# Two mixers of a tuned TensorE-bound kernel: the softmax by four heads at a time, and ten taps and a split behind the first scores

## The chip, the core and the metric

The kernel runs on one core of a Trainium2 chip. The metric is the device time of one execution in microseconds. Before the change three runs took 2920.37, 2922.01 and 2922.98 us, so the median is 2922.01 us. The engines are named as in the profile: PE is TensorE (PEld its weight loads), DVE is VectorE, ACT is ScalarE, POOL is GpSimd, SP is SyncE, which issues most of the weight transfers.

## What is computed

The program is two networks in a row: a block of depth 2 (each layer: feed-forward, mixer, feed-forward) on 512 tokens of width 1024, and then a second block with a scan, a gated mixer and sixteen experts. The change touches the mixer of the first block alone, which runs twice. Cut to what matters:

```python
u = x @ w_in
u_conv, u_lru, q, k, v = jnp.split(u, [o1, o2, o3, o4], axis=-1)
y_conv = _conv_module(u_conv, ...)      # gate, 31 causal taps, layernorm, silu
y_lru = _recurrent(u_lru, ...)          # short conv, gates, scan, gelu gate
y_attn = _swa(q, k, v, ...)             # 8 heads, blocks of 128, window 128
return jnp.concatenate([y_conv, y_lru, y_attn], axis=-1) @ w_out

# _swa, per block of 128 queries, over this block of keys and the one before
s = einsum('bnqgrd,bnkgd->bngrqk', qb, kb) * (HEAD_DIM ** -0.5) + band_bias
s = where(valid, s, -1e30)
p = softmax(concatenate([s, sink], axis=-1))[..., :-1]
o = einsum('bngrqk,bnkgd->bnqgrd', p, vb)
```

The output projection needs all three parts, and the four query blocks of the attention are independent of each other.

## The kernel before

Every large product runs on TensorE as three matmuls of split operands (high by high, high by low, low by high). Weights come through one stream in order of use: SP loads 512 KB pieces into a ring of four buffers (`raw`); ACT copies a piece to its high part (`whl`, line 81) and DVE subtracts to get the low part (line 82), which frees the buffer. The stream also carries `ada_w`, weights of the second network, which need no split: eight steps of `mod` (line 853), each of two pieces and four matmuls, are spread over the mixer as filler, and a piece's buffer is free when its second matmul has read it.

The mixer goes as follows. Fourteen projections (`pj`) give the inputs. DVE works off a list of 62 taps of the convolution (`tap`, line 372, in place on `acc`) in portions that `drain(n)` takes, between the splits of q (`ql`, line 406), the recurrence (`hs`) and its split into the operand of the output projection (`split_to`, lines 631 and 632). Then come the four query blocks. `scores(b)` makes two pairs of score banks (`sc`, line 461; `rp` 0 holds heads 0 to 3, `rp` 1 heads 4 to 7); DVE adds the bias, and takes the maximum with the sink, head by head (line 468, tile `S`); then for all eight heads at once the negated maximum (471) and the sink's difference (472); ACT does eight exponentials with row sums (475) and the sink's (476); DVE adds and takes the reciprocal (477, 478); the heads are normalized by turns on DVE (484) and ACT (482). `pv(b)` transposes the heads (`tp`, 496) for each of the block's key blocks, has ACT copy group 0 (`pT`, 501) and DVE group 1 (`pT`, 499), multiplies by v (`yv`, 506, one instruction for each group), and splits the result (`xTh` on ACT, 511; `xTl` on DVE, 512). Block 0 has one key block, the others two. The convolution's layernorm (`conv_ln`: `cn`, `bn`, `mv`, a square root on ACT with its table load in `rs`, `nt`, `cb`, `yc`) and the last `pv` run beside the output projection (`down`, line 220, bank `dn`, 12 matmuls for each of its half steps).

The text of the program isn't the order of the engines: a scheduler orders each engine's instructions by its own estimates of their durations, and each engine then runs its list strictly as it stands; what it estimates wrong shows as a wait. The code calls `scores(0)`, `scores(1)`, `pv(0)`, `scores(2)`, `pv(1)`, `scores(3)`, the first steps of `conv_ln`, `pv(2)`, and leaves the rest of `conv_ln` and `pv(3)` to `down`.

Of the kernel before, what the change touches and what calls it, by code (L numbers as in the profile page):

```python
# [10 lines left out]
AF = mybir.ActivationFunctionType  # L11
OP = mybir.AluOpType
# [86 lines left out]
class Kernel:  # L99
# [237 lines left out]
    def mixer(self, l, st, pb, ln, nxt):  # L337
        nc, w = self.nc, self.w
# [77 lines left out]
        lru = {}  # L416
# [29 lines left out]
        def scores(b):  # L446
            k0 = 0 if b else 128
            ks = slice((b - 1) * 128 if b else 0, (b + 1) * 128)
            n = 256 - k0
            st = self.mp.tile([128, 5, 8], F32, tag="sm", name="sm", bufs=4)  # L450
            s = {}
            sink = self.sinks[:, l]
            bs = slice(b * 128, b * 128 + 128)
            for rp in range(2):
                ps = [self.ps("sc").rearrange("p (r k) -> p r k", r=2) for _ in range(2)]
                for rr in range(2):
                    for n_m in range(3):
                        for g in range(2):
                            hs = slice(g * 64, g * 64 + 64)
                            lq, rk = ((self.qh, self.kh), (self.qh, self.kl), (self.ql, self.kh))[n_m]  # L460
                            nc.tensor.matmul(ps[g][:, rr, :n], lq[hs, 2 * rp + rr, bs], rk[hs, ks], start=(n_m == 0),
                                             stop=(n_m == 2))
                for g in range(2):
                    t = mun(name="S").rearrange("p (r k) -> p r k", r=2)
                    for rr in range(2):
                        r = 2 * rp + rr
                        h = 2 * r + g
                        nc.vector.tensor_tensor_reduce(t[:, rr, k0:], ps[g][:, rr, :n], self.bias[:, r, g, k0:], 1.0,
                                                       sink[:, h:h + 1], op0=OP.add, op1=OP.max, accum_out=st[:, 0, h:h + 1])
                    s[rp, g] = t  # L470
            nc.vector.tensor_scalar(st[:, 1], st[:, 0], -1.0, None, op0=OP.mult)
            nc.vector.tensor_tensor(out=st[:, 2], in0=sink, in1=st[:, 0], op=OP.subtract)
            for h in range(8):
                sv = s[h // 4, h % 2][:, h // 2 % 2, k0:]
                nc.scalar.activation(sv, sv, AF.Exp, bias=st[:, 1, h:h + 1], accum_out=st[:, 3, h:h + 1])
            nc.scalar.activation(st[:, 2], st[:, 2], AF.Exp)
            nc.vector.tensor_tensor(out=st[:, 3], in0=st[:, 3], in1=st[:, 2], op=OP.add)
            nc.vector.reciprocal(st[:, 4], st[:, 3])
            for h in range(8):
                sv = s[h // 4, h % 2][:, h // 2 % 2, k0:]  # L480
                if h % 2:
                    nc.scalar.activation(sv, sv, AF.Copy, scale=st[:, 4, h:h + 1])
                else:
                    nc.vector.tensor_scalar(sv, sv, st[:, 4, h:h + 1], None, op0=OP.mult)
            sc[b] = s

        def pv(b):
# [86 lines left out]
        for r in range(4):  # L574
            pj(10 + r)
            post_q(r)
            self.drain(6)
            if r == 0:
                v_nat()
        for c in range(2):  # L580
            self.split_to(c, lru[c])
        per = PER
        run = lambda *gs: [0 for g in gs for _ in g]
        scores(0)
        self.drain(5)
        self.mod(per)
        scores(1)
# [1470 lines left out]
```

## Time and profile before

| | us |
|---|---|
| median of three runs | 2922.01 |
| the profiled execution | 2918.46 |
| its span, first to last instruction | 2916.7 |
| PE busy | 2863.8 (98%) |
| DVE busy | 1333.1 (46%) |
| ACT busy | 1004.5 (34%) |

A row of the timeline has a start in us from the span's start, a duration, engine, line, operation, tile written and read, shape and count; in brackets stands how long the engine was idle before it, and what ended that. Durations of successive instructions overlap, so the pace is the step from one start to the next. Matmuls of fp32 leave two records each, so `x4` in the trace is two instructions of the order. The first mixer's attention lies at 464 to 525 us, the second's 922.8 us later, at 1387 to 1448.

### The profile page before, as it was taken

Reading aid. Unit: us, or ns where it says so; the run is one execution under the profiler, and the core shown is the slowest. Engines: PE = TensorE matmul, PEld = TensorE weight load, DVE = VectorE, ACT = ScalarE, POOL = GpSimd, SP = SyncE. Lnnn points to the kernel's source line nnn. Section 1 sums busy time; section 2 is a strip of 40 time slices with the busy share of each in tenths; the row PEclk is TensorE's granted clock in tenths of the full one; section 3 lists DMA queues with packets and bytes.
Section 4 is the critical chain, followed back from the end, with each engine's and each line's share of the span. In section 5 each row is a group of like instructions: output and inputs, shape, how many; then the busy total and the mean of one; then the engine's idle time right before and its main releaser. Section 6 shows DMA issues by size and latency. Waiting matters only on the chain.

```text
span 2916.7 us, 35208 instructions
## 1 busy us (share of the span) xinstructions
PE 2863.8 (98%) x14404; PEld 2196.4 (75%) x14404; DVE 1333.1 (46%) x2259; ACT 1004.5 (34%) x1591; POOL 37.7 (1%) x63
## 2 busy tenths in 40 slices
PE   8999998999999999999899999999999999999998
PEld 7888885888888878888588888878878886544453
DVE  4223398533334333359653334778863453222223
ACT  4222355422224122344552223567742321100011
POOL 0000000000000000000100000000000000000000
PEclk9999999999999999999999999999999999999999
DMA  6432334333223354232633323232244357899998
GB/s 197 114 101 74 96 116 150 97 112 108 94 80 95 95 191 137 80 108 70 200 109 98 104 80 103 89 115 80 88 138 137 94 202 281 342 406 426 426 427 329
DMA packets 104257, 465.91 MB, mean 160 GB/s; under 512 B 12837, under 2 KB 13493, under 8 KB 79520
## 3 DMA queue, kind: packets, MB, share of 16 engines
q1 hardware_dynamic: 95936, 435.81, 41.7%
q0 software_dynamic: 6720, 23.13, 2.8%
q10 hardware_dynamic: 1440, 4.72, 0.4%
q8 instruction: 113, 1.85, 0.3%
q14 instruction: 48, 0.39, 0.0%
HBM read 457.73 MB, written 5.88 MB: 159 GB/s over the span
## 4 chain that ended last, share of the span: by engine, by line
PE 84%; DVE 7%; DMA 5%; ACT 2%; issue 1%; SPq 0%; DVEq 0%; ACTq 0%
PE dn L220 19%; PE pg L114 6%; PE pg L115 6%; PE pg L116 6%; PE pu L116 5%; PE pu L114 5%; PE pu L115 5%; DMA er<-in_eu 3%; PE ey L1671 3%; PE pj L115 3%; PE pj L116 3%; PE pj L114 3%; PE eu L1671 2%; PE eg L1671 2%; PE ga L1671 2%; PE wo L1455 2%
## 5 line engine op out<-in xcount | busy, mean ns | idle before, releaser
L82 DVE TENSOR_TENSOR whl<-raw,whl 128x1024 fp32r<-128x1024 f32 (+1 forms) x385 | 468.6, 1221 | 692.0 <-ACT whl L81 691.7
L81 ACT ACTIVATE whl<-raw 128x1024 fp32r<-128x1024 f32 (+1 forms) x385 | 405.9, 1056 | 659.8 <-PE pu L116 249.8
L220 PE MATMUL dn<-whl,hhl 128*128 128x512 f32 x2112 | 492.9, 395 | 0.0
L220 PEld LDWEIGHTS dn<-whl,hhl 128*128 128x128 f32 x2112 | 397.5, 188 | 92.3
L114 PE MATMUL pg<-xTh,whl 128*128 128x512 f32 x768 | 300.3, 391 | 0.0
L116 PE MATMUL pg<-xTh,whl 128*128 128x512 f32 x768 | 298.9, 389 | 0.0
L115 PE MATMUL pg<-xTl,whl 128*128 128x512 f32 x768 | 298.8, 389 | 0.0
L114 PE MATMUL pu<-xTh,whl 128*128 128x512 f32 x704 | 274.7, 390 | 0.7 <-ACT whl L81 0.7
L115 PE MATMUL pu<-xTl,whl 128*128 128x512 f32 x704 | 273.9, 389 | 0.0
L116 PE MATMUL pu<-xTh,whl 128*128 128x512 f32 x704 | 273.7, 389 | 0.0
L114 PE MATMUL pj<-xTh,whl 128*128 128x256 f32 (+1 forms) x688 | 230.7, 335 | 0.0
L116 PE MATMUL pj<-xTh,whl 128*128 128x256 f32 (+1 forms) x688 | 224.8, 327 | 0.0
L115 PE MATMUL pj<-xTl,whl 128*128 128x256 f32 (+1 forms) x688 | 224.5, 326 | 0.0
L114 PEld LDWEIGHTS pg<-xTh,whl 128*128 128x128 f32 x768 | 144.2, 188 | 36.8 <-issue 7.4
L116 PEld LDWEIGHTS pg<-xTh,whl 128*128 128x128 f32 x768 | 144.1, 188 | 30.3
L115 PEld LDWEIGHTS pg<-xTl,whl 128*128 128x128 f32 x768 | 144.2, 188 | 29.3
L290 ACT ACTIVATE sg<-pg 128x512 f32<-128x512 f32 x80 | 47.8, 597 | 320.8 <-PE pg L116 320.8
L114 PEld LDWEIGHTS pu<-xTh,whl 128*128 128x128 f32 x704 | 132.1, 188 | 28.6 <-ACT whl L81 1.1
L116 PEld LDWEIGHTS pu<-xTh,whl 128*128 128x128 f32 x704 | 132.2, 188 | 27.6
L115 PEld LDWEIGHTS pu<-xTl,whl 128*128 128x128 f32 x704 | 132.1, 188 | 27.5 <-issue 0.2
L293 DVE SCALAR_TENSOR_TENSOR h<-sg,pu 128x512 f32<-128x512 f32 x74 | 50.8, 687 | 198.2 <-PE pu L116 198.2
L115 PEld LDWEIGHTS pj<-xTl,whl 128*128 128x128 f32 x688 | 131.4, 191 | 10.9 <-issue 0.5
(483 smaller groups left out, 3855.3 us busy)
## 6 DMA issues: line engine op xcount, KB each, us to landing
raw<-in_wgu SPq DMA_DIRECT2D x176, 512.0 KB, 3.6
er<-in_eu SPq DMA_DIRECT2D x64, 1024.0 KB, 18.9
er<-in_eg SPq DMA_DIRECT2D x64, 1024.0 KB, 18.2
er<-in_ed SPq DMA_DIRECT2D x56, 1024.0 KB, 19.1
raw<-in_wd SPq DMA_DIRECT2D x88, 512.0 KB, 3.5
raw<-in_win SPq DMA_DIRECT2D x76, 512.0 KB, 3.6
raw<-in_ada_w SPq DMA_DIRECT2D x48, 512.0 KB, 4.7
raw<-in_wout SPq DMA_DIRECT2D x16, 512.0 KB, 4.6
```

The lines of the kernel that those rows point to most:

```text
L81: k.nc.scalar.activation(hi, r, AF.Copy)
L82: k.nc.vector.tensor_tensor(out=lo, in0=r, in1=hi.bitcast(F32), op=OP.subtract)
L114: mm(out, l[0], r[0], start=start, stop=False)
L115: mm(out, l[0], r[1], start=False, stop=False)
L116: mm(out, l[1], r[0], start=False, stop=stop)
L220: nc.tensor.matmul(banks[t, dh], l[:, s], r[:, dh * 512:(dh + 1) * 512], start=(u == 0 and n_l == 0), stop=(u == last and n_l == 2))
L290: nc.scalar.activation(sg, pg, AF.Silu)
L293: return nc.vector.scalar_tensor_tensor(h, sg, 0.5, pu, op0=OP.mult, op1=OP.mult)
L1455: nc.tensor.matmul(banks[t, dh], mg[k][l][:, s], wo[k][dh][r], start=(k == 0 and n == 0), stop=(k == 7 and n == 2))
L1671: return tc.keep_in_program_order(nc.tensor.matmul(*args, **kw))
```

## The change

The softmax of a block is now done inside the loop over `rp`, for four heads at a time: negated maximum, sink's difference, four exponentials, sum, reciprocal and normalization for heads 0 to 3 and again for heads 4 to 7. The portions that `drain` takes behind the four q projections go from 6, 6, 6, 6 to 6, 6, 0, 0, so ten taps are still on the list when `scores(0)` is called, and `split_to` of the recurrence is called behind `scores(0)`. Nothing else is changed; lines behind the loop move by two.

```diff
-            nc.vector.tensor_scalar(st[:, 1], st[:, 0], -1.0, None, op0=OP.mult)
-            nc.vector.tensor_tensor(out=st[:, 2], in0=sink, in1=st[:, 0], op=OP.subtract)
-            for h in range(8):
...
+                hs = slice(4 * rp, 4 * rp + 4)
+                nc.vector.tensor_scalar(st[:, 1, hs], st[:, 0, hs], -1.0, None, op0=OP.mult)
+                nc.vector.tensor_tensor(out=st[:, 2, hs], in0=sink[:, hs], in1=st[:, 0, hs], op=OP.subtract)
+                for h in range(4 * rp, 4 * rp + 4):
+                    sv = s[rp, h % 2][:, h // 2 % 2, k0:]
+                    nc.scalar.activation(sv, sv, AF.Exp, bias=st[:, 1, h:h + 1], accum_out=st[:, 3, h:h + 1])
+                nc.scalar.activation(st[:, 2, hs], st[:, 2, hs], AF.Exp)
+                nc.vector.tensor_tensor(out=st[:, 3, hs], in0=st[:, 3, hs], in1=st[:, 2, hs], op=OP.add)
+                nc.vector.reciprocal(st[:, 4, hs], st[:, 3, hs])
+                for h in range(4 * rp, 4 * rp + 4):
...
             post_q(r)
-            self.drain(6)
+            self.drain((6, 6, 0, 0)[r])
...
-        for c in range(2):
-            self.split_to(c, lru[c])
...
         scores(0)
+        for c in range(2):
+            self.split_to(c, lru[c])
         self.drain(5)
```

In the scheduled program PE, DVE and ACT change between the last q projection and the end of the attention, in the same way in both mixers; outside these stretches their orders are the same as before, and SP's is the same throughout.

**Block 0.** DVE at the last q split and the first scores (`ISA S,sm` is line 468 of one head, `acc` a tap, whose number of columns counts down to 482 for the last one), before:

```order
L406 SCALAR_TENSOR_TENSOR ql<-pj,qh 128x512
L372 SCALAR_TENSOR_TENSOR acc<-yin,pc,acc 128x488
L372 SCALAR_TENSOR_TENSOR acc<-yin,pc,acc 128x487
L372 SCALAR_TENSOR_TENSOR acc<-yin,pc,acc 128x486
L468 ISA S,sm<-sc,bias,sinks 128x128
L468 ISA sm 128x1
L372 SCALAR_TENSOR_TENSOR acc<-yin,pc,acc 128x485
```

DVE at the same place now, the q split first:

```order
L406 SCALAR_TENSOR_TENSOR ql<-pj,qh 128x512
L372 SCALAR_TENSOR_TENSOR acc<-yin,pc,acc 128x489
L372 SCALAR_TENSOR_TENSOR acc<-yin,pc,acc 128x488
L372 SCALAR_TENSOR_TENSOR acc<-yin,pc,acc 128x487
L468 ISA S,sm<-sc,bias,sinks 128x128
```

and at the end of the first four heads:

```order
L468 ISA sm 128x1
L372 SCALAR_TENSOR_TENSOR acc<-yin,pc,acc 128x486
L473 TENSOR_SCALAR sm<-sm 128x4
L474 TENSOR_TENSOR sm<-sinks,sm 128x4
L372 SCALAR_TENSOR_TENSOR acc<-yin,pc,acc 128x485
```

The q split stands one tap earlier, the recurrence's split still stands ahead of it, and of the ten taps five still stand ahead of the scores and five stand between and behind them. PE behind the scores of block 1 up to block 0's product with v, before:

```order
L853 MATMUL mod<-raw,cs 32x512 x9
L496 MATMUL tp<-ident,S 128x128 x7
L853 MATMUL mod<-raw,cs 32x512
L496 MATMUL tp<-ident,S 128x128
L853 MATMUL mod<-raw,cs 32x512 x6
L506 MATMUL yv<-pT,vn 64x512 x2
```

and now:

```order
L855 MATMUL mod<-raw,cs 32x512 x4
L498 MATMUL tp<-ident,S 128x128 x4
L855 MATMUL mod<-raw,cs 32x512
L498 MATMUL tp<-ident,S 128x128 x4
L855 MATMUL mod<-raw,cs 32x512 x8
L508 MATMUL yv<-pT,vn 64x512 x2
```

Five of the filler's matmuls that stood ahead of block 0's transposes now stand between or behind them.

**Block 2.** PE behind the scores of block 3 (`cn` the convolution's transposes, the first `tp` and `yv` those of block 2's first key block), before:

```order
L524 MATMUL cn<-ident,acc 128x128 x4
L496 MATMUL tp<-ident,S 128x128 x8
L506 MATMUL yv<-pT,vn 64x512
L524 MATMUL cn<-ident,acc 128x128 x2
L496 MATMUL tp<-ident,S 128x128
L524 MATMUL cn<-ident,acc 128x128 x2
L496 MATMUL tp<-ident,S 128x128 x7
L220 MATMUL dn<-whl,xTh 128x512 x2
```

and now:

```order
L526 MATMUL cn<-ident,acc 128x128 x4
L498 MATMUL tp<-ident,S 128x128 x8
L526 MATMUL cn<-ident,acc 128x128 x4
L508 MATMUL yv<-pT,vn 64x512 x2
L498 MATMUL tp<-ident,S 128x128 x8
L220 MATMUL dn<-whl,xTh 128x512
L508 MATMUL yv<-pT,vn 64x512
L220 MATMUL dn<-whl,xTh 128x512 x2
L508 MATMUL yv<-pT,vn 64x512
```

The second `yv` of block 2's first key block stood behind 17 matmuls of the output projection (not shown) and stands now ahead of all of them; the pair of its second key block stood behind 24 and stands behind one and three. ACT at this place (the first `pT` is block 1's second key block, the second one block 2's first; `S,sm` x8 are the exponentials of block 3), before:

```order
L501 ACTIVATE pT<-tp 128x512
L81 ACTIVATE whl<-raw 128x1024
L482 ACTIVATE S<-S,sm 128x256 x4
L511 ACTIVATE xTh<-yv 128x4x128
L81 ACTIVATE whl<-raw 128x1024 x2
L501 ACTIVATE pT<-tp 128x512
L81 ACTIVATE whl<-raw 128x1024
L475 ACTIVATE S,sm<-S,sm 128x256 x8
L476 ACTIVATE sm<-sm 128x8
L530 ACT_TABLE_LOAD
L530 ACTIVATE rs<-mv,eps_100 128x4
```

and now, from the split of block 1's product to block 2's first copy:

```order
L513 ACTIVATE xTh<-yv 128x4x128
L81 ACTIVATE whl<-raw 128x1024 x3
L477 ACTIVATE S,sm<-S,sm 128x256 x4
L478 ACTIVATE sm<-sm 128x4
L477 ACTIVATE S,sm<-S,sm 128x256 x3
L484 ACTIVATE S<-S,sm 128x256 x2
L477 ACTIVATE S,sm<-S,sm 128x256
L478 ACTIVATE sm<-sm 128x4
L532 ACT_TABLE_LOAD
L532 ACTIVATE rs<-mv,eps_100 128x4
L503 ACTIVATE pT<-tp 128x512
```

Block 2's first copy moved from ahead of block 3's exponentials to behind them, the table load and the square root; five of the output projection's weight copies stand ahead of those exponentials, where there were four.

## Rows read from the trace of the kernel before

**Rows 1.** Stretches of both mixers: length, each engine's busy time, PE clock, DMA share, GB/s.

```profile
463.90:510.70 46.80, 38.95 (x245) 19.83 (x243) 36.23 (x129) 32.83 (x100) 4.51 (x7) 0.93 0.70 234
1386.70:1433.50 46.80, 37.90 (x245) 19.22 (x243) 36.01 (x129) 32.16 (x99) 3.59 (x6) 0.96 0.71 232
530.00:550.00 20.00, 20.00 (x92) 16.56 (x91) 8.22 (x16) 8.49 (x13) 0.00 (x0) 1.00 0.26 79
```

**Rows 2.** Timeline of PE, first mixer.

```profile
470.63 0.38 PE L461 MATMUL sc<-kh,qh 64*128 64x256 f32 x1 [0.99 <-DVE sm L468]
...
478.08 1.30 PE L853 MATMUL mod<-raw,cs 128*32 128x512 f32 x2 [3.06 <-DMA raw<-in_ada_w]
...
484.63 1.08 PE L506 MATMUL yv<-pT,vn 128*64 128x512 f32 x4
...
491.65 1.08 PE L506 MATMUL yv<-pT,vn 128*64 128x512 f32 x4
492.66 1.09 PE L496 MATMUL tp<-ident,S 128*128 128x128 f32 x8
...
501.77 1.15 PE L506 MATMUL yv<-pT,vn 128*64 128x512 f32 x2 [2.62 <-DVE sm L472]
...
523.07 1.93 PE L506 MATMUL yv<-pT,vn 128*64 128x512 f32 x6
...
526.42 1.09 PE L220 MATMUL dn<-whl,xTh 128*128 128x512 f32 x4
527.35 0.62 PE L220 MATMUL dn<-whl,xTl 128*128 128x512 f32 x2
```

**Rows 3.** Timeline of ACT, first mixer.

```profile
474.63 0.40 ACT L475 ACTIVATE S<-S,sm 128x128 f32<-128x128 f32 x1 [8.01 <-DVE sm L471]
...
501.14 0.58 ACT L501 ACTIVATE pT<-tp 128x512 f32<-128x512 f32 x1
501.84 1.06 ACT L81 ACTIVATE whl<-raw 128x1024 fp32r<-128x1024 f32 x1
502.80 0.49 ACT L475 ACTIVATE S<-S,sm 128x256 f32<-128x256 f32 x1
...
506.74 0.19 ACT L476 ACTIVATE sm<-sm 128x8 f32<-128x8 f32 x1
506.95 1.28 ACT L530 ACT_TABLE_LOAD   x1
508.24 0.30 ACT L530 ACTIVATE rs<-mv,eps 128x4 f32<-128x4 f32 x1
508.47 1.71 ACT L482 ACTIVATE S<-S,sm 128x256 f32<-128x256 f32 x4
```

**Rows 4.** Timeline of DVE, first mixer.

```profile
467.16 2.24 DVE L372 SCALAR_TENSOR_TENSOR acc<-yin,pc,acc 128x488 f32<-128x488 f32 x3
...
473.75 0.35 DVE L468 CUSTOM_DVE_ANT_0 S<-sc,bias,sinks 128x128 f32<-128x128 f32 x1
...
474.02 0.48 DVE L468 CUSTOM_DVE_ANT_0 S<-sc,bias,sinks 128x256 f32<-128x256 f32 x1
...
487.06 0.69 DVE L512 TENSOR_TENSOR xTl<-yv,xTh 128x512 fp32r<-128x512 f32 x1
487.67 0.47 DVE L468 CUSTOM_DVE_ANT_0 S<-sc,bias,sinks 128x256 f32<-128x256 f32 x1
```

**Rows 5.** DMA issues, 460 to 530 us: KB each, median us from issue to landing.

```profile
raw<-in_ada_w SPq DMA_DIRECT2D x12, 512.0 KB, 5.5
raw<-in_wout SPq DMA_DIRECT2D x8, 512.0 KB, 4.5
```

**Rows 6.** Timeline of PE, second mixer.

```profile
1423.33 1.11 PE L506 MATMUL yv<-pT,vn 128*64 128x512 f32 x2 [2.07 <-ACT pT L501]
...
1445.90 1.93 PE L506 MATMUL yv<-pT,vn 128*64 128x512 f32 x6
```

**Rows 7.** A stretch as in rows 1, behind PE's wait at 501.77.

```profile
501.80:506.20 4.40, 4.40 (x16) 3.38 (x17) 3.91 (x10) 4.36 (x15) 1.38 (x3) 0.61 0.75 222
```

More of the change, by code (lines that the diff above doesn't have):

```diff
@@ L470, in scores @@
                     s[rp, g] = t
-            nc.vector.tensor_scalar(st[:, 1], st[:, 0], -1.0, None, op0=OP.mult)
-            nc.vector.tensor_tensor(out=st[:, 2], in0=sink, in1=st[:, 0], op=OP.subtract)
-            for h in range(8):
[L474 to L484, printed above, removed]
+                hs = slice(4 * rp, 4 * rp + 4)
[8 more added lines that the diff above has]
+                for h in range(4 * rp, 4 * rp + 4):
+                    sv = s[rp, h % 2][:, h // 2 % 2, k0:]
+                    if h % 2:
+                        nc.scalar.activation(sv, sv, AF.Copy, scale=st[:, 4, h:h + 1])
+                    else:
+                        nc.vector.tensor_scalar(sv, sv, st[:, 4, h:h + 1], None, op0=OP.mult)
             sc[b] = s
```

## Prediction, made before the changed kernel ran

> **What bounds the kernel now.** I read the page's busy times first: PE is busy for nearly the whole span, so only a stretch in which PE stands still can give or take time. Then the stretches of the two attentions: PE is busy for 38.95 and 37.90 of 46.80 us there, so 7.85 + 8.90 = 16.75 us are idle, while 20 us behind them are full at a granted clock of 1.00 [rows 1]. Whatever PE loses in an attention is not made up behind it. Then PE's timeline in these 46.8 us, for who ends each wait: a bank that DVE frees (0.99 us), a filler piece from memory (3.06 us), and 2.62 us ahead of block 2's first product with v [rows 2]. The last is put down to DVE, but ACT's copy of that block's transposes ended at 501.14 + 0.58 = 501.72, just ahead of 501.77 [rows 2, 3], and the second mixer names that copy (2.07 us) [rows 6]. So the question is when ACT comes to each `pT`, and for that I walk PE, DVE and ACT through the new order with the steps of the old rows.
>
> **The change part by part.** Steps, from one start to the next: three taps in a row 2.24 us, so 0.75 each (0.65 with another instruction between, by its share of the overlap), a head's scores on DVE 0.27 (128 columns) and 0.40 (256), a small step taken as 0.1, xTl 0.61 and a copy taken as the same [rows 4]; on ACT an exponential with its sum 0.39 (128 columns, a little under the 0.40 shown) and 0.49 (eight from 502.80 to 506.74), two normalizations 0.8, a weight copy 0.96, a `pT` 0.5 of its 0.58, the table load 1.29, the root 0.23 [rows 3]; on PE two `yv` 1.0, eight `tp` 1.0, a matmul of the projection 0.23 (four from 526.42 to 527.35) [rows 2].
>
> *Added instructions.* A block has one negation, difference, sum, reciprocal and sink exponential more: four on DVE of 0.1 us, one on ACT of 0.1. That is 2 us of DVE and 0.4 us of ACT for a mixer, in stretches where DVE is busy for 36.23 and ACT for 32.83 of 46.80 us [rows 1]; I take them into the walk and nothing beside it.
>
> *The ten taps and the split.* The order undoes most of this: five taps and the whole split still stand ahead of the first scores, and one tap of 0.65 us and three that stood between the first heads go behind them. Cost on the path nothing; gain in the next step.
>
> *Block 0, gain.* Tap 487 ends at about 468.7 as before [rows 4]. Four heads to 469.8, a tap, negation and difference: ACT starts its exponentials at 470.6, not 474.63 [rows 3], 4.0 us earlier. PE's 0.99 us for the bank goes, since the two heads that free it are done at 469.2 [rows 2].
>
> *Block 0, what takes the place.* PE now has four filler matmuls, four transposes, one filler matmul, four transposes and eight filler matmuls in a row. Heads 0 to 3 are normalized at 475.2 on DVE (a tap, heads 4 to 7, two taps, two heads of block 1 and the small steps stand between), heads 4 to 7 at 477.1. So the filler piece that PE read behind the third wait of old is read at 478.2, its buffer is free only then, and the next piece for it lands 4.3 us later at 482.5; I stay just under the lower of the two medians, 5.5 and 4.5, since nothing queues ahead of it [rows 5]. ACT, by 16 exponentials, its sinks and six normalizations, ends block 0's `pT` at 482.7. Both let `yv` start at 482.8, not 484.63: of 4.0 us gained 1.8 are left.
>
> *Block 1, loss.* The next DVE scores stand behind xTl of block 0 (484.55 to 485.15); five heads and a negation later, at 487.4, ACT starts block 2's eight exponentials, and now they, with two normalizations and sinks, stand ahead of block 1's `pT`: 487.4 + 3.9 + 0.8 + 0.2 + 0.5 = 492.8. Its `yv` starts at 492.9, not 491.65 [rows 2]. The last filler pieces land at 491 to 492 by the same ring, so they don't decide.
>
> *Block 2, the main term.* Transposes 1.0, DVE's copy 0.6, `yv` of the second key block 495.6 to 496.6, the scores of block 3 around it; DVE then does a weight split to 497.85, xTl 0.6, five heads 2.0, negation 0.15: block 3's exponentials may start at 500.6. But ACT's fifth weight copy stands ahead of them. Its buffer is freed by DVE's split of the first piece at 496.7; it lands 4.3 us later at 501.0, and is copied at 502.0. From there ACT has eight exponentials 3.9, sinks 0.2, two normalizations 0.8, table load 1.29, root 0.23 and `pT` 0.5: 6.9 us (with the steps between engines, 7.0). `yv` of block 2 starts at **509.0**, where it started at 501.77 [rows 2]. PE has run out by 500 (the other `cn` and the transposes are done), so it stands for some 9 us where it stood for 2.62.
>
> *Sum.* The common point of both orders is the end of the last `yv`, 523.07 + 1.93 = 525.0 [rows 2], with all scores, transposes and 48 matmuls of the projection done in both. Of old it took 23.2 us from 501.77 to there. The new order has the same left but four `cn` (0.45): 509.0 + 22.8 = 531.8, **6.8 us late**. Counted at full pace instead (eight `yv` 4.0, 24 `tp` 3.0, 48 matmuls 11.0, eight `cb` as eight `tp` 1.0) with one stretch at the lower clock, 1.7 (below), and two waits of about 0.45 for the next copies on ACT and DVE it is 21.6: 530.6, **5.6 us late**. I take the lower, since the old 23.2 us hold more switches between kinds of matmul. The old common point of the second mixer lies at 1447.83, which is 525.0 + 922.8 [rows 2, 6]: the same loss there. Together 11.2 us. The profiled execution took 2918.46 us, 3.6 below the median; the difference goes on the median: 2922.0 + 11.2 = **2933.2 us**. Bounds for a mixer: if the fifth weight copy is no gate, ACT starts at 500.6, 1.4 less (4.2 late); if that piece takes the 5.5 us of the filler, 1.2 more, and with the 6.8 of the other count 8.0 late. Twice that is 8.4 to 16.0.
>
> *The clock.* Behind the wait of 2.62 us the granted clock was 0.61 over 4.4 us [rows 7]. 0.61 means 78% of 4.4 us at 1.2 instead of 2.4 GHz, so 1.7 us lost. My sum has one such loss behind the long wait, which the old time has too. The Trainium skill, "TensorE: Matmul & The Clock Gate", section on HAM oscillation, speaks against this change: bursts of matmuls between waits run at the lower clock each time, not once. By it block 1's products and transposes behind their waits would lose too, some 1.7 us more for each mixer and 2936.6 in all; the old trace shows it behind one wait of 2.62 us, and says nothing of shorter ones.
>
> *The table load.* It takes 1.28 us here, the next instruction starts 1.29 us after its start, and the sink's exponential ends at 506.93 as it starts [rows 3]. The Trainium skill, "ScalarE: Activation LUTs", section "What ACT_TABLE_LOAD costs", adds a drain of 1.38 us to each switch. With it the sum would be 2.8 us more; the row shows no drain, and I leave it out.
>
> **The rivals.**
> 1. *Faster: the half softmax carries through.* Mechanism: ACT is ahead by the 4.0 us of block 0 and keeps it, so that block 2's `pT`, though behind block 3's exponentials, comes before 501.8. Place: that `yv`. For it: the waits on DVE and ACT, 0.99 + 2.62 here and 2.07 in the second mixer [rows 2, 6], and 1.7 for the clock in each, could all go; 16.75 us are idle at most [rows 1]. It would need block 3's exponentials to start at 494.8; of old they started at 502.80 [rows 3]. A gain decides from a start below 496.4 on, 5.6 us ahead of mine, since then the common point comes early. About 4 us for each mixer: 2914.
> 2. *No difference.* The filler and weight pieces come faster than I have it and DVE's small steps overlap, so the exponentials start at about 498.5: `yv` at 505.5, 2.1 us late at the common point, 2922.0 + 4.2 = 2926. For it: the medians of 5.5 and 4.5 us are of transfers with others in flight [rows 5], and a lone one may land sooner. Against it: the scores, xTl and the copies ahead of that start are DVE's and ACT's own steps, and no transfer shortens them.
> 3. *Slower still.* The lower clock at each burst, and a late weight piece: 8 to 10 us for each mixer, 2940.
> 4. *The change doesn't do what it says.* For taps and split that holds already by the order; the half softmax is in the order, so this has no chance of its own.
>
> **How the numbers follow.** The forecast, 2927 to 2938, has 0.60; rival 3, 0.12; rival 2, 0.18; rival 1, 0.10. A measurement here can tell about 0.2%, 5.8 us, from no change. Faster is rival 1, 0.10; within is rival 2, 0.18, and 0.02 of the forecast's low end; slower is the rest, 0.70. The range reaches from inside rival 2 to the upper bound and part of rival 3: 2921 to 2942.
>
> **What would show it.** In the profile after: ACT's exponentials of block 0 at 470 to 471; the wait for the filler piece ahead of block 0's `yv` still there, but at 480 to 482; block 1's `yv` later than 491.65; and one wait of PE of 7 to 10 us ahead of block 2's `yv` in each mixer, ended by ACT's `pT`, with the table load just ahead of that copy; PE full from there on. The fifth weight copy should show a wait on its transfer. It is wrong if that wait is under 4 us, if ACT's copy is done before PE asks for it, or if PE makes up time behind 531.

## The result, and the profile of the changed kernel

The changed kernel takes 2950.1 us (median of four runs, 2946.75 to 2951.1) against 2922.49 for the kernel before on the same chip: 1.0094 times as long, 95% interval 1.0079 to 1.011. A second set of runs on another chip gave 2947.72 us, 1.0091 (1.0076 to 1.0106). It is slower, as forecast, but by 27 us and not by 11, and it lies above the range. The profiled execution has a span of 2948.3 us (2916.7 before) and a mean granted clock of 0.989 (0.996 before).

The first two stretches answer to [rows 1], the others are pieces of the first mixer (columns: length, busy us of PE, PEld, DVE, ACT, POOL, granted clock, DMA share, GB/s):

```profile
463.90:510.70 46.80, 33.52 (x214) 14.44 (x212) 31.22 (x120) 25.54 (x78) 0.73 (x1) 0.85 0.61 206
1386.70:1433.50 46.80, 37.53 (x231) 22.71 (x229) 39.56 (x120) 21.62 (x72) 0.00 (x0) 0.95 0.39 139
...
475.40:480.30 4.90, 4.89 (x21) 1.76 (x24) 4.45 (x25) 3.92 (x18) 0.73 (x1) 0.65 0.20 84
497.70:502.00 4.30, 4.27 (x12) 0.67 (x12) 0.96 (x4) 3.52 (x11) 0.00 (x0) 0.50 0.97 356
518.50:522.50 4.00, 3.95 (x13) 2.33 (x13) 4.00 (x6) 3.30 (x5) 3.05 (x4) 0.50 0.80 223
526.50:542.00 15.50, 15.50 (x79) 11.38 (x79) 5.09 (x11) 4.58 (x7) 0.00 (x0) 1.00 0.08 32
```

In the first mixer PE is busy for 5.4 us less of the same 46.8 us, and the granted clock is 0.85 where it was 0.93. The second mixer starts later by what the first one lost, so its row is not level with the old one; its waits, below, are the better reading. From 526.5 us on PE is full at a clock of 1.00, as forecast: nothing is made up. From its first filler step to the end of its last `yv` a mixer took 60.4 us before, both times; now it takes 76.5 and 74.0, so the first loses 16.1 us and the second 13.6, in single executions.

PE's timeline of the first mixer, for [rows 2]:

```profile
475.41 0.74 PE L498 MATMUL tp<-ident,S 128*128 128x128 f32 x4 [3.10 <-DVE S L486]
...
486.54 1.91 PE L855 MATMUL mod<-raw,cs 128*32 128x512 f32 x2 [5.39 <-DMA raw<-in_ada_w]
488.38 1.83 PE L508 MATMUL yv<-pT,vn 128*64 128x512 f32 x4
...
497.73 3.17 PE L855 MATMUL mod<-raw,cs 128*32 128x512 f32 x8 [3.02 <-DMA raw<-in_ada_w]
500.83 1.98 PE L508 MATMUL yv<-pT,vn 128*64 128x512 f32 x4
...
518.55 2.28 PE L508 MATMUL yv<-pT,vn 128*64 128x512 f32 x4 [6.04 <-ACT pT L503]
...
540.51 1.08 PE L508 MATMUL yv<-pT,vn 128*64 128x512 f32 x4
```

ACT's timeline, for [rows 3], two rows of the start and the place ahead of block 2's products:

```profile
471.06 0.40 ACT L477 ACTIVATE S<-S,sm 128x128 f32<-128x128 f32 x1 [3.99 <-DVE sm L473]
...
482.66 0.57 ACT L503 ACTIVATE pT<-tp 128x512 f32<-128x512 f32 x1
...
510.43 1.06 ACT L81 ACTIVATE whl<-raw 128x1024 fp32r<-128x1024 f32 x1 [1.82 <-DMA raw<-in_wout]
511.39 0.49 ACT L477 ACTIVATE S<-S,sm 128x256 f32<-128x256 f32 x1
...
516.22 0.19 ACT L478 ACTIVATE sm<-sm 128x4 f32<-128x4 f32 x1
516.42 1.28 ACT L532 ACT_TABLE_LOAD   x1
517.72 0.30 ACT L532 ACTIVATE rs<-mv,eps 128x4 f32<-128x4 f32 x1
517.92 0.58 ACT L503 ACTIVATE pT<-tp 128x512 f32<-128x512 f32 x1
```

The waits and the order that the forecast named are there: the early exponentials (471.06), the copy of block 0 at 482.66 (forecast 482.7, as its end), a wait on a filler piece ahead of block 0's `yv`, the fifth weight copy that waits on its transfer, and a long wait ahead of block 2's `yv` with the table load just ahead of the copy that ends it. That wait is 6.04 us, under the 7 to 10 that were named. And block 0's `yv` is at 488.4 and not at 482.8, block 1's at 500.8 and not at 492.9, and the last `yv` ends at 541.6 and not at 530.6. The chain of what ended last shows how block 0's filler piece came (start, us, what): it is asked for when PE has read the piece whose buffer it takes, and it lands 6.18 us later.

```profile
478.89 1.43 PE mod L855 x7
480.31 6.18 DMA raw<-in_ada_w
```

In the second mixer the long wait is 9.8 us. PE's waits between 1400 and 1482 us (total, times, longest), the answer to [rows 6]:

```profile
PE yv L508 <- ACT pT L503: 9.8, 1, 9.8
PE mod L855 <- DMA raw<-in_ada_w: 6.1, 2, 3.2
PE tp L498 <- DVE S L486: 3.0, 1, 3.0
PE cn L526 <- DVE bn L527: 2.3, 1, 2.3
```

There the fifth weight piece is the late one. The chain and GpSimd's timeline of the second mixer show that it lands 8.22 us after its request (4.29 in the first mixer, forecast 4.3), and that the filler's bias was asked for 3 us ahead of it:

```profile
1439.59 8.22 DMA raw<-in_wout
...
1436.53 0.74 POOL L863 DMA_DIRECT2D ab<-in_ada_b  x1
```

### The profile page after: what moved, and what is told of

Read it like the earlier page. It is cut to its first block, busy times and chain, and to the rows that moved or that the text cites. A ratio compares the mean times of both kernels' runs of the same rounds, so it can differ in the third digit from the quotient of the medians.

```text
span 2948.3 us, 35252 instructions
## 1 busy us (share of the span) xinstructions
PE 2870.4 (97%) x14404; PEld 2198.2 (75%) x14404; DVE 1336.2 (45%) x2291; ACT 1006.9 (34%) x1599; POOL 37.7 (1%) x63
## 4 chain that ended last, share of the span: by engine, by line
PE 84%; DVE 7%; DMA 6%; ACT 2%; issue 1%; SPq 0%; DVEq 0%; ACTq 0%
PE dn L220 19%; PE pg L114 6%; PE pg L116 6%; PE pg L115 6%; PE pu L116 5%; PE pu L114 5%; PE pu L115 5%; DMA er<-in_eu 3%; PE ey L1673 3%; PE pj L115 3%; PE pj L116 3%; PE pj L114 3%; PE eu L1673 2%; PE eg L1673 2%; PE ga L1673 2%; PE wo L1457 1%
## 5 line engine op out<-in xcount | busy, mean ns | idle before, releaser
L220 PE MATMUL dn<-whl,hhl 128*128 128x512 f32 x2112 | 492.9, 395 | 0.0
```

Source lines behind the costliest of these rows:

```text
L220: nc.tensor.matmul(banks[t, dh], l[:, s], r[:, dh * 512:(dh + 1) * 512], start=(u == 0 and n_l == 0), stop=(u == last and n_l == 2))
```

## The experiments

All times are ratios of a kernel to the kernel before on the same chip, so that runs on different chips can be set side by side.

| kernel | median us | ratio, 95% interval |
|---|---|---|
| changed | 2950.1 | 1.0094 (1.0079 to 1.011) |
| changed, again | 2947.7 | 1.0091 (1.0076 to 1.0106) |
| taps and split alone | 2921.6 | 1.0007 (0.9997 to 1.0017) |
| softmax by four heads alone | 2946.7 | 1.0093 (1.0078 to 1.0108) |
| changed, block 2's copy first | 2928.7 | 1.0028 (1.0017 to 1.0039) |
| changed, no filler loads | 2940.2 | 1.0072 (1.0057 to 1.0087) |
| no filler loads, idle products (too long) | 2983.4 | 1.021 (1.0193 to 1.0227) |
| no filler loads, short idle products | 2931.3 | 1.0034 (1.0021 to 1.0046) |
| copy first and no filler loads | 2918.5 | 0.9989 (0.9979 to 0.9998) |
| copy first, four filler steps early | 2928.9 | 1.0027 (1.0017 to 1.0037) |
| changed, filler's bias loaded early | 2941.5 | 1.0067 (1.0052 to 1.0082) |
| copy first and bias early | 2921.4 | 0.9998 (0.9989 to 1.0007) |
| before, bias early | 2919.6 | 0.9995 (0.9986 to 1.0004) |
| four heads in block 0 alone | 2940.4 | 1.0062 (1.0047 to 1.0077) |
| four heads in blocks 0 and 1 | 2932.1 | 1.0035 (1.0022 to 1.0048) |
| block 0 alone, bias early, two filler steps early | 2918.5 | 0.9988 (0.998 to 0.9997) |
| block 0 alone, bias early, four filler steps early | 2921.6 | 0.9999 (0.999 to 1.0007) |

**Which half of the change.** The kernel before with the taps and the split moved, and then with the softmax's lines alone:

> Only the first half of the change: the ten taps and the recurrence's split are written behind block 0's scores, the softmax goes by eight heads as before. Theory A (all of the loss comes with the softmax by four heads; the taps stay beside other work): within 0.15% of the kernel before, 2918 to 2927 us, and PE's waits in the attentions as before (6.0 us on filler pieces, 5 to 6 us on block 2's pT). Rival B (the moved taps delay the split and the conv's transposes, and this is part of the loss): 2930 us or more, with a wait on DVE ahead of the conv's transposes. Rival C (the early scores alone are a gain): under 2916 us.

> Only the second half of the change: the softmax by four heads, taps and split as before. Theory A: nearly the whole loss, 2944 to 2952 us, with the same long waits ahead of block 2's products with v in both mixers (6 to 10 us each, ended by ACT's pT). Rival B (the loss needs the moved taps too): under 2935 us.

The taps and the split cost nothing that can be told (1.0007), the softmax by four heads costs all (1.0093). In the second kernel the filler waits are small, and PE's order of filler and transposes ahead of block 0's `yv` is another one; PE waits for ACT's copies instead, though for no longer than 4.6 us at once where theory A had 6 to 10. Its waits of 455 to 545 us:

```profile
PE yv L508 <- ACT pT L503: 9.4, 4, 4.6
...
PE mod L855 <- DMA raw<-in_ada_w: 1.7, 3, 1.3
```

So the waits on filler pieces are not needed for a loss of this size. That is a warning for the experiments below: idle time that is taken away in one place can stand in another.

**The copy's place.**

```diff
+        p2 = pv(2)
+        next(p2)
+        with self.tc.issue_after(self.pt_ins.ins):
-        scores(3)
+            scores(3)
...
-        run(pv(2))
+        run(p2)
```

> The changed kernel, with one thing put back: the transposes of block 2's first key block are written ahead of block 3's scores, and ACT's copy of them stands ahead of block 3's exponentials. Theory A (the wait of 6.0 and 9.8 us ahead of block 2's products with v is made by ACT's order, and PE has work behind it): both waits shrink to under 3 us, and 8 to 15 us come back: 2935 to 2942 us. Rival B (the filler ring sets the pace, and PE would stand elsewhere for the next weight pieces or for the convolution's norm): under 4 us come back, 2946 to 2950 us, with new waits of several us on the weights or on DVE behind block 2's products.

It gave back more than either theory had it: 1.0028. PE's timeline there, at the same place:

```profile
505.65 1.08 PE L508 MATMUL yv<-pT,vn 128*64 128x512 f32 x4 [0.16 <-DVE xTl L514]
...
508.22 0.73 PE L220 MATMUL dn<-whl,xTh 128*128 128x512 f32 x2 [0.29 <-DVE sm L468]
```

Block 2's first `yv` starts at 505.65 where it started at 518.55, and PE goes straight on to the projection (`dn`), so the exponentials of block 3 run beside it. The wait was 6.04 us, but block 2's `yv` comes 12.9 us earlier: with the copy behind the exponentials, `yv` also stood behind the weight copy's transfer and the whole exponential chain. The main term's mechanism is shown: with the copy's place the wait goes and the time comes back (the edit also brings forward block 2's transposes on PE, which the copy needs). The waits on filler pieces are still there in this kernel (7.0 and 6.2 us).

**The filler's transfers.** The filler's matmuls read a resident tile, and the pieces for them in the two mixers are left out:

```diff
-        r0, r1 = w.get(u), w.get(u + 1)
+        r0, r1 = (w.get(u), w.get(u + 1)) if u is not None else (self.x[0], self.x[0])
```

> The changed kernel without the filler's transfers in the two mixers: the filler's matmuls read a resident tile in place of the sixteen pieces of weights, which aren't loaded (so the rows that they make are not those of the reference); every matmul stays. Theory A (the terms that were sized too small are the filler ring: 14.5 us of waits on pieces, and the late fifth weight piece): block 0's products with v start at 482 to 484, block 1's at 492 to 494, block 3's exponentials at 500 to 502, a wait of 6 to 9 us on block 2's pT stays in each mixer; 2928 to 2935 us. Rival B (what PE doesn't wait for pieces, it waits ahead of block 2's pT): 2943 us or more, with that wait grown to over 10 us in each mixer.

Between the two theories: 1.0072, some 6 us back of 27. The walk's early steps come near their places (block 0's `yv` at 483.98 for 482.8, block 1's at 495.05 for 492.9), but block 3's exponentials start at 504.68 although the weights are long there, and the last `yv` ends at 536.25 and not at 530.6. PE's timeline behind the two waits on ACT's copies:

```profile
495.05 1.98 PE L508 MATMUL yv<-pT,vn 128*64 128x512 f32 x4 [6.20 <-ACT pT L503]
496.96 1.97 PE L498 MATMUL tp<-ident,S 128*128 128x128 f32 x8
...
512.64 1.98 PE L508 MATMUL yv<-pT,vn 128*64 128x512 f32 x4 [5.41 <-ACT pT L503]
...
519.40 1.07 PE L508 MATMUL yv<-pT,vn 128*64 128x512 f32 x2 [1.10 <-DVE pT L501]
```

Two products take 1.98 us and eight transposes 1.97, about twice the 1.1 that I took from [rows 2]. The granted clock there, in parts of full speed, is at its lower level of 1.2 GHz (0.50) or near it:

```profile
494.40:502.00 7.60, 6.95 (x32) 3.61 (x34) 1.80 (x6) 2.70 (x7) 0.00 (x0) 0.60 0.00 0
509.80:516.00 6.20, 3.35 (x11) 1.75 (x12) 1.65 (x6) 3.08 (x6) 4.04 (x6) 0.50 0.34 61
```

**Is the lower clock on the path?** To answer this PE gets products in its waits that serve nothing:

```diff
+    def idle(self, bank):
+        self.nc.tensor.matmul(bank[0:32], self.cs[:, 0], self.x[0][:, 0:512], start=True, stop=True, skip_group_check=True)
...
+                for _ in range({1: 22, 2: 18}.get(b, 0) if kb == 0 else 0):
+                    self.idle(y)
```

> The changed kernel without the filler's transfers (as in the run without them), and with products that serve nothing, 22 ahead of block 1's first product with v, 18 ahead of block 2's and 7 ahead of the second half of the convolution's transposes, into banks that are written anew behind them. They stand where PE waited 6.2, 5.4 and 2.2 us, so the waits shrink and PE is busy until the operands come. Theory A (TensorE's lower clock behind each wait is on the path): the granted clock behind block 1's wait goes from about half to near 1.00, two products with v take 1.1 instead of 2.0 us and eight transposes 1.1 instead of 2.0, block 3's exponentials start 1.5 to 3 us earlier, and 4 to 10 us come back against the run without the transfers: 2930 to 2936 us. Rival B (the lower clock falls beside ACT's and DVE's steps): within 3 us of that run, 2937 to 2943 us, or longer by what of the products doesn't fit the waits.

This failed by my sizing: 1.021. Of the 22 products 21 stand in a row and take 18.2 us, where 5 were reckoned for all. The trace shows the filler's matmuls in fours, each into another group of 32 rows of a bank, and twelve of them in 2.78 us; one after another into the same rows they take 0.87 us each. The second try is a quarter as wide (128 columns), without those at the convolution's transposes, and with a line that holds the transposes of blocks 1 and 2 behind their first `yv`, as in the kernel without loads:

> The changed kernel without the filler's transfers (its rows are then not those of the reference), and with products that serve nothing: the run with idle products once more, with products a quarter as wide, since a full one took 0.87 us and not the 0.23 that was reckoned (18.2 us for the 22 ahead of block 1's product in place of 5). By that, 22 take 4.7 us and 18 take 3.9, and stand in waits of 6.2 and 5.4 us, in an order of the engines that is else that of the run without the transfers. Theory A (TensorE's lower clock behind the wait is on the path): behind block 1's wait two products with v take 1.1 instead of 2.0 us and eight transposes 1.1 instead of 2.0, block 3's exponentials start 1.5 to 3 us earlier, the same behind block 2's wait, and 4 to 10 us come back against the run without the transfers: 1.004 to 1.006 of the kernel before. Rival B (the lower clock falls beside steps of ACT and DVE that set the pace): 1.0065 to 1.0085.

Here it is 1.0034, against 1.0072 without them: products that compute nothing give back 11 us by the two ratios, whose intervals leave 5 to 17. The same rows as above, in this kernel:

```profile
494.44 1.08 PE L518 MATMUL yv<-pT,vn 128*64 128x512 f32 x4 [0.76 <-ACT pT L511]
495.45 1.09 PE L501 MATMUL tp<-ident,S 128*128 128x128 f32 x8
...
509.87 1.08 PE L518 MATMUL yv<-pT,vn 128*64 128x512 f32 x4 [2.88 <-ACT pT L511]
```

```profile
494.40:502.00 7.60, 7.49 (x58) 4.86 (x58) 4.19 (x17) 2.21 (x5) 0.00 (x0) 1.00 0.00 0
509.80:516.00 6.20, 6.11 (x27) 3.44 (x28) 3.26 (x7) 2.49 (x4) 3.58 (x4) 1.00 0.21 5
```

The clock is 1.00 behind both waits, though a wait of 2.88 us is left ahead of the second, and the products take 1.08 us again. Theory A holds: the lower clock is on the path. Its size is less sure. In the traces the first mixer is 5.3 us shorter and the second 1.7, so 7 us in the two, and of the first mixer's 5.3 us 1.1 are the wait on DVE's copy at 519.40 above, which this kernel, with another order of DVE there, doesn't have in that mixer. What the rest of the 11 us is stays open. And it was shown without the filler's loads; the changed kernel with idle products wasn't run.

**Do the two causes add up?**

> Both edits on the changed kernel: block 2's first copy of the transposes ahead of block 3's exponentials, and no transfers for the filler (its rows are then not those of the reference). Theory A (the two causes add up: about 20 us by the first alone, 6 to 10 us by the second alone): 2918 to 2923 us, level with the kernel before. Rival B (they are the same idle time, seen twice): 2926 us or more.

> The changed kernel with block 2's first copy ahead of block 3's exponentials, and three more of the filler's eight steps put into the projection ahead of the attention (four there, four in the attention). Theory A (the waits of 7.0 and 6.2 us on filler pieces in the two mixers are worth more than the 3.2 us of products that the fuller projection gets): 2919 to 2925 us. Rival B (PE then waits as long for ACT's copies, since the filler was what it did meanwhile): 2927 to 2935 us.

Without the loads and with the copy first it is 0.9989, level with before or a little under it: the two add up. With the copy first, bringing the filler forward in place of leaving out its loads (three more steps in the projection) gave nothing over the copy alone, 1.0027: PE then waits for ACT's copies (7.0 us in the first mixer, 11.9 in the second), as rival B said, while the projection gets the filler on top.

**Why the pieces land late.** In the changed kernel GpSimd asks for the filler's bias just ahead of the late pieces; the issues of 478 to 500 us and that request (the last column of an issue is the median time to landing):

```profile
raw<-in_ada_w SPq DMA_DIRECT2D x6, 512.0 KB, 6.6
```

```profile
479.05 0.73 POOL L863 DMA_DIRECT2D ab<-in_ada_b  x1 [76.13 <-PE tp L498]
```

```diff
             st["ps"] = self.ps("mod")
+            st["ab"] = ab = self.unit(name="ab")
...
+            nc.gpsimd.dma_start(ab, src)
```

> The changed kernel with GpSimd's load of the filler's bias (256 KB, in packets under 512 bytes, issued at 479.05 us, just ahead of the pieces that took 6.2 to 8.4 us to land) put ahead of the attention, where the filler's first step stands. The orders of PE, ACT and DVE in the attention stay but for a few scores. Theory A (those small packets hold up the filler pieces): the piece for block 0 lands in 4.3 to 5 us, PE's waits on pieces fall from 14.5 to under 10 us in the two mixers, and 3 to 6 us come back: 1.007 to 1.008. Rival B (the pieces are slow because six of them are asked for within 2 us, after a burst of the filler): the waits stay within 2 us of 14.5, 1.0085 to 1.010.

With the request at 403.2 us the same six pieces land in 4.5 us, the wait ahead of block 0's `yv` is 2.84 and not 5.39 us, and the time is 1.0067, 7 to 8 us back, more than theory A's 3 to 6:

```profile
raw<-in_ada_w SPq DMA_DIRECT2D x6, 512.0 KB, 4.5
```

```profile
484.29 1.04 PE L859 MATMUL mod<-raw,cs 128*32 128x512 f32 x2 [2.84 <-DMA raw<-in_ada_w]
```

But PE's waits on pieces fell from 14.5 to 11.9 us only, not under 10. The rest has another cause beside it, which the text of the edit doesn't show: the scheduler ordered ACT anew, so that four weight copies (three in the second mixer) stand ahead of block 3's exponentials where there were five, and ACT waits for no weight piece there. In the changed kernel it waited 1.82 us for the fifth in the first mixer (510.43, above) and in the second:

```profile
1447.83 1.06 ACT L81 ACTIVATE whl<-raw 128x1024 fp32r<-128x1024 f32 x1 [4.70 <-DMA raw<-in_wout]
```

So in the second mixer nearly all that came back came by way of this copy: counted from the mixer's first filler step, block 1's `yv` is 0.8 us earlier there, block 3's exponentials 6.2. How much of it is the bias's transfer and how much the new order was not told apart, nor whether it is the packets' size or only the queues' share. Two runs set this beside the other cause and beside the old order:

> The changed kernel with block 2's first copy ahead of block 3's exponentials and the filler's bias loaded ahead of the attention. Theory A (the two causes add up): 19 and 7 us come back, 0.999 to 1.001 of the kernel before, 2918 to 2924 us. Rival B (with the copy in front, the late pieces are waited for beside something else): 1.002 to 1.003, as with the copy alone.

> The kernel before with the filler's bias loaded ahead of the attention, nothing else. Theory A (in the old order PE's waits for pieces are 6.0 us in all, and the bias is asked for at 481.22, behind most of them): within 0.1% of the kernel before. Rival B (the small packets cost the old order as much as the new): 0.997 to 0.9985, 4 to 8 us less, and then they are no part of the difference between the two kernels.

With both edits, and nothing left out, the loss is gone: 0.9998. In the kernel before the bias's place makes no difference that can be told (0.9995). So two edits undo the loss: a copy that no longer stands behind the next block's exponentials, and a bias asked for ahead of the attention, with what the scheduler made of it (here too fewer weight copies stand ahead of block 3's exponentials).

**Does block 0's early start carry through?**

> The changed kernel with the softmax by four heads in block 0 alone; blocks 1 to 3 go by eight heads, as before. In the order ACT's copy of block 0's transposes then stands ahead of block 1's exponentials, and block 2's first copy ahead of block 3's. Theory A (the loss comes from the later blocks' half exponentials standing ahead of copies; block 0's early start is worth its 4 us where no copy is displaced): block 0's exponentials at 470 to 471, its products with v by 480 instead of 484.6, no wait of over 3 us ahead of block 2's, and 2 to 8 us less than before: 2912 to 2919 us. Rival B (the filler ring and the later blocks take up what block 0 gains): 2919 to 2925 us, within 0.15% of before. Rival C (the split softmax itself costs): over 2930 us.

> The changed kernel with the softmax by four heads in blocks 0 and 1. In the order block 1's exponentials then stand ahead of block 0's copy, but block 1's copy ahead of block 2's exponentials and block 2's first copy ahead of block 3's. Theory A (what costs is a copy behind the next block's exponentials; of three such places one is left): block 0's products with v about as late as in the changed kernel, no long wait ahead of block 2's, and a time between the kernel before and the one with block 2's copy first: 2921 to 2929 us. Rival B (the loss is there from the first two blocks on): 2935 us or more.

Block 0 alone took 1.0062, which by number is rival C's, but not by what the trace shows: theory A's mechanism worked as far as block 2, whose first `yv` starts at 500.00 in it, earlier than the 501.77 of [rows 2]; but then PE waits for the projection's weights, 3.49 us for copies that ACT does only behind block 3's exponentials, the table load and four normalizations, and 2.62 us for a split that stands on DVE behind a step which waits for a transfer of the filler's result. In the second mixer it waits 10.2 us for the bank that the filler's sum holds, until DVE has added the bias, and DVE waits for the bias's transfer. Its timeline of PE, then a row of its waits from 1385 to 1490 us and DVE's row:

```profile
500.00 1.07 PE L514 MATMUL yv<-pT,vn 128*64 128x512 f32 x2 [0.25 <-ACT pT L509]
...
510.88 0.96 PE L221 MATMUL dn<-whl,xTh 128*128 128x512 f32 x3 [3.49 <-ACT whl L82]
```

```profile
PE dn L221 <- DVE ab L870: 10.2, 1, 10.2
...
1443.81 0.69 DVE L870 TENSOR_TENSOR ab<-ab,mod 128x512 f32<-128x512 f32 x1 [10.08 <-DMA ab<-in_ada_b]
```

With blocks 0 and 1 it is 1.0035; the long wait ahead of block 2 (5.1 and 3.1 us) is half gone, where theory A had none, and a filler wait of 6.1 us is there. It took 2932 us, between theory A (2921 to 2929) and rival B (2935 and more). Two more runs take those limits away:

> The changed kernel with the softmax by four heads in block 0 alone, the bias loaded ahead of the attention, and one more of the filler's eight steps in the projection (two there, six in the attention). Theory A (block 0's early start carries through to block 2 once the weights behind the filler come in time): no wait of over 2 us on weights or on the filler's bank behind block 2's products, 0.997 to 0.9995 of the kernel before, 2913 to 2920 us. Rival B (what is won at block 0 is waited for again at the weights): 1.001 to 1.006.

> As the run beside it, with four of the filler's eight steps in the projection. The weights come earlier still, and PE has four steps (4.2 us) less to fill its waits in the attention with, which the full projection gets on top. Theory A (weights were the limit): 0.997 to 0.9995. Rival B (with the weights in time, ACT's copies are the limit, and the filler is missed): 1.000 to 1.003, with waits on ACT's copies of 5 us and more.

The first is 0.9988 (0.998 to 0.9997), 2.6 us less than before by the medians and 3.5 by the ratio: the only kernel here with nothing left out whose interval ends below 1, though by less than the 0.2% that I called the limit of one comparison, and one of seventeen intervals. The kernel before with the same places of bias and filler was not run, so it isn't shown that block 0's early start is what gains; it does show that the split softmax need not cost anything (rival C above). Its waits of 455 to 545 us:

```profile
PE tp L504 <- DVE S L470: 4.3, 2, 3.7
PE yv L514 <- ACT pT L509: 2.0, 3, 0.8
PE dn L221 <- DVE whl L83: 1.6, 2, 0.9
```

The wait on DVE's normalization ahead of block 0's transposes is what block 0's early softmax has in place of the old ones. With four filler steps early it is 0.9999, level, between theory A and rival B; no wait on ACT's copies there is over 2.5 us, where rival B had 5 and more.

## Why the direction was right and the size wrong

The walk's steps, in us from the first filler step of the first mixer (which starts at 464.61 before, 465.06 changed, 465.15 without loads, 463.83 with idle products):

| step | forecast | changed | no loads | no loads, idle products |
|---|---|---|---|---|
| exponentials of block 0 | 6.0 | 6.0 | 6.9 | 6.9 |
| `yv` of block 0 | 18.2 | 23.3 | 18.8 | 19.8 |
| `yv` of block 1 | 28.3 | 35.8 | 29.9 | 30.6 |
| exponentials of block 3 | 37.4 | 46.3 | 39.5 | 38.1 |
| `yv` of block 2 | 44.4 | 53.5 | 47.5 | 46.0 |
| end of the last `yv` | 66.0 | 76.5 | 71.1 | 65.8 |
| the same, second mixer | 66.0 | 74.0 | 68.7 | 67.1 |

Where pieces don't land late and the clock mostly stays up, the walk ends within 0.3 us of the forecast in the first mixer and 1.1 in the second. That is in part luck: this kernel has neither the late fifth weight piece nor the stretch at the lower clock that the forecast counts, 1.4 and 1.7 us, and without them the forecast would end at 62.9. Up to block 2's `yv` the walk was some 3 us short (46.0 for 43.0, which is 44.4 less the 1.4), 1.6 of them by block 0, where the clock was 0.51 behind a wait of 3.88 us that got no idle products; behind block 2's `yv` the count was right (19.8 for 19.9). So the order and the waits were right, and two terms were sized far too small. Of the 27 us some 6 go with the filler's loads by the ratios (1.0093 to 1.0072) and 11 with the lower clock (to 1.0034); the traces of the two mixers put it the other way, 11 of 30 with the loads and 7 with the clock. By either count 17 to 18 go with the two together, and 10 to 12 are left, where the forecast had 11.2 in all.

- *Added instructions; the ten taps and the split.* "Cost on the path nothing": right, 1.0007 with these alone.
- *Block 0, gain.* Right: 471.06 for 470.6, the bank wait down from 0.99 to 0.19 us.
- *Block 0, what takes the place.* This step failed. ACT's copy ended block 0 as forecast, but the filler piece was read at 480.3 and not at 478.2, since the matmuls behind the wait of 3.10 us ran at a clock of 0.65, and the next one landed 6.2 us later and not 4.3. "Nothing queues ahead of it" left two things out: SP asks for four pieces within 2.2 us there, and the bias goes beside them. I had both medians [rows 5] and went just under the lower.
- *Block 1, loss.* That the last filler pieces "don't decide" failed: the last filler piece ended PE's wait at 497.73, ACT's copy was done at 499.37, and both came some 6 to 7 us late.
- *Block 2, the main term.* Mechanism and length right: from block 3's exponentials to the end of the wait 7.2 us (511.39 to 518.55), forecast 7.0; the weight copy waits for its transfer just ahead. In the first mixer the exponentials started 9.4 us late with what stands ahead of them. In the second the landing was the mis-sized term: 8.22 us for 4.3, so that "the same loss there" came about by another late piece.
- *The clock.* The other mis-sized term. I counted 1.7 us once for a mixer, behind the long wait, by a wait of 2.62 us [rows 7], and called that the one place where the old trace shows the lower clock. It shows it behind the 3.06 us of the first mixer and the 2.07 us of the second too:

```profile
478.10:482.50 4.40, 4.40 (x11) 1.66 (x11) 1.09 (x6) 4.36 (x18) 0.73 (x1) 0.61 0.45 176
1423.40:1428.00 4.60, 4.60 (x18) 3.56 (x18) 2.84 (x11) 4.60 (x17) 1.09 (x2) 0.63 0.77 207
```

In the changed kernel the granted clock behind waits of 3 to 6 us is 0.50 to 0.65 at three places of the first mixer, and from block 2's `yv` to the end it is 23.6 us without loads and 19.7 with the clock up; 1.1 of these 3.9 us are the wait on DVE's copy, and in the second mixer it is 21.3 and 20.9. The Trainium skill, "TensorE: Matmul & The Clock Gate", section on HAM oscillation, says that bursts between waits run at the lower clock each time; the first mixer without loads agrees (1.98 against 1.08 us for two products), but it is not so each time: behind the wait of 3.17 us in the changed kernel's second mixer the granted clock was 1.00, and there the measurement decides:

```profile
1423.18 1.04 PE L855 MATMUL mod<-raw,cs 128*32 128x512 f32 x2 [3.17 <-DMA raw<-in_ada_w]
...
1423.20:1427.00 3.80, 3.80 (x32) 2.02 (x33) 1.06 (x4) 0.60 (x1) 0.00 (x0) 1.00 0.81 315
```

With the 1.7 us more for each mixer that I priced by it, and left out, the clock comes to 6.8 us in the two mixers; what idle products gave back is 7 by the traces and 11 by the times, with the lower clock still there at block 0.
- *The table load.* Right: the instruction ahead ends at 516.41, the load takes 1.28 us from 516.42 on, the next starts at 517.72. The drain of 1.38 us that the Trainium skill, "ScalarE: Activation LUTs", section "What ACT_TABLE_LOAD costs", adds is not in the row, and the row decides.
- *Sum.* The lower of two counts for the rest, 21.6 us behind block 2's `yv`, held in the first mixer where the clock stayed up (19.7, to which the 1.7 for the clock is to be added); in the changed kernel it was 23.0.
- *Rivals.* Rival 3 was the case, by its own two mechanisms: the clock at several bursts, and a late weight piece, which the second mixer has; its 2940 was too low by 8 to 10 us. Rival 1 may show in part once the limits behind it are gone (0.9988), but what gains there isn't told apart.

## What to carry to other kernels

A softmax in smaller parts starts earlier, but on an engine that works in order each part that comes sooner stands ahead of a copy that another engine waits for: ask, for each block, what the new start displaces, and hold the copies in front where the scheduler doesn't. Where matmul's engine waits for some microseconds at several places, price the lower clock at each of them, with the work behind each at half pace, and look for all such places in the trace of before; if that work is on the path, harmless products in the wait can give time back (7 to 11 us here). A filler whose pieces come through a small ring is no free cover: moved into a burst, it waits for its own transfers, and these land later beside others (6.6 us against 4.5). And where a scheduler orders the engines, compare the orders after each edit: moving one load moved weight copies too, and what came back can't be put down to the load alone.

## What the runs showed of the hardware

- The granted clock behind a wait of 6.20 us was 0.60 over 7.6 us; with idle products in that wait it was 1.00. With such products in two waits of each mixer 7 us came back in the two mixers by the traces, 11 of the whole by the times.
- Not every wait of that length is followed by the lower clock: behind the changed kernel's 3.17 us on a filler piece (second mixer) it was 1.00.
- A product of 32 columns by 512, in plain 32-bit floats, takes 0.87 us when the next goes into the same rows of a bank; four into four groups of rows take about 0.93 together (twelve in 2.78 us).
- One load of 256 KB in small packets, asked for beside six pieces of 512 KB, goes with a median landing of 6.6 us for these (7.5 in the changed kernel's second profile), against 4.5 with that load elsewhere.
